# An SSM's tap matrix in eight transfers a layer instead of 32, and the rows of w_glu and p_ssm in two transfers a chunk, in another channel order

## The chip, the cores and the metric

The kernel runs on one core of one Trainium2 chip, in one launch. The metric is the device time of that launch in microseconds. All inputs lie in HBM at the start, in float32, and the output (1, 256, 1024) is written there.

## What is computed

Two post-norm decoder layers over 256 positions of width 1024. In each layer a hybrid mixer (an S5 state-space branch with a GLU, beside a sparse attention) and a SwiGLU feed-forward of width 2816, both modulated by a conditioning vector. The S5 branch has 32 groups of 16 channels and 64 complex states; w_glu is 512 x 512, p_ssm 512 x 1024. The change lies in this branch and in how these two weights are read for it. Cut to what matters:

```python
def s5_branch(u, lam_re, lam_im, log_dt, b_re, b_im, c_re, c_im, d_skip, w_glu, b_glu):
    uf = u.astype(f32).reshape(bsz, L, SSM_GROUPS, SSM_GROUP)
    ...
    _, _, hr, hi = lax.associative_scan(combine, (a_r, a_i, xr, xi), axis=1)
    y = (jnp.einsum('bsgp,gip->bsgi', hr, c_re.astype(f32))
         - jnp.einsum('bsgp,gip->bsgi', hi, c_im.astype(f32))
         + d_skip.astype(f32).reshape(SSM_GROUPS, SSM_GROUP) * uf)
    y = jax.nn.gelu(y.reshape(bsz, L, SSM_WIDTH))
    y = y * jax.nn.sigmoid(y @ w_glu.astype(f32) + b_glu.astype(f32))
    return y

def hybrid_mixer(u, ...):
    z = u @ w_in
    ...
    merged = jax.nn.sigmoid(g_ssm) * (y_ssm @ p_ssm) + jax.nn.sigmoid(g_attn) * (y_attn @ p_attn)
    return merged @ w_out
```

## The kernel before, in words

**Weights.** Nearly all of the time is matmuls with weights that are read once. SP issues the loads on one queue, in chunks of 512 KB: `w_in` as 128 partitions x 2 x 512, `w_cond` (for the modulation) as 128 x 1024. A class `Stream` holds the order of all chunks; `pump_dma` (L334) issues a chunk once one of six raw buffers is free, and `advance` (L354) has the chunks split, two ahead of the one in use. A chunk is split into a high part (ACT's cast, L388) and the rest (DVE's subtraction, L389), and PE multiplies three of the four products of parts: L1355 where the weights are the moving side, L1431 where they are stationary. `w_cond` goes to PE unsplit (L476). The order of PE's instructions is that of the program text; the order on ACT, DVE, POOL and SP is made by a scheduler from priorities and its own estimates, and is fixed in the program. Each engine takes its list strictly in order, and so does SP with its DMAs; a DMA waits on SP until the eighth one before it has landed.

**The S5 branch** (`ssm_run`, L762). Time is cut into 32 blocks of T = 8 positions. Groups are numbered by k (0 to 3, a block of 32 partitions) and m (0 to 7). Inside a block the output follows from the inputs of the block by a small Toeplitz matrix, the *taps*; between blocks a scan of states runs on DVE (L834 and L835 transpose for it on PE, L505 and L506 swap halves by DMA). `ssm_tables` leaves the kernel of the recurrence in an SBUF tile `KT`, 128 partitions x 1920, of which 16 rows of each 32 are channels. It is written to a DRAM copy `KT_d` in one transfer of 960 KB (L797), and read back into the tap matrix `MT` (128 rows: position s and channel j; then m, k and 128 columns) with an offset that shifts by 16 columns with s. That is `taps_in` (L799): for each k and each s one transfer of 16 partitions x 8 x 128, 64 KB in pieces of 512 bytes (L805), 32 a layer. PE uses `MT` at L865, after the scan (L861). Before it, `rope` (the input of the branch) is written to the tile `s` by 16x8x128 transfers from SBUF (L774) on SP's and ACT's queues.

Then GELU (L869 to L875), whose last product on DVE writes `yg` in the order t, m, i (i is the channel of a group), PE's transposes of it (L885), ACT's copy of them (L886, which writes with a stride of eight elements), the split into `yy` (L227 and L893), and the GLU on PE (`glu`, L896, matmuls L910 to L912).

**w_glu and p_ssm.** Their rows have to stand in the order of the transposes, so a chunk of theirs is read with `w_rows_perm` (L402) in eight transfers of 16 partitions x 2 x 512, 64 KB each (L349): 32 for w_glu and 64 for p_ssm in both layers. The columns of w_glu are permuted as well, by the split of such a chunk (ACT L384, DVE L385). The bias of the GLU is transposed from `bg4` (L530) into the same order.

**Beside it**, on PE: L821 (states into the blocks), L1011 (scores of the attention's indexer, from copies that ACT makes with L227), ACT's L1014 (their activation), L1044 and L1057 (further steps of the attention).

Of the kernel before, what the change touches and what calls it, by code (L numbers as in the profile page):

```python
# [8 lines left out]
F32 = mybir.dt.float32  # L9
# [14 lines left out]
T = 8  # L24
# [148 lines left out]
def kernel(  # L173
# [10 lines left out]
    dp = ctx.enter_context(tc.tile_pool(name="dp", bufs=1, space=DRAM))  # L184
    V, A, P, PE, SP = nc.vector, nc.scalar, nc.gpsimd, nc.tensor, nc.sync
# [21 lines left out]
    def nm(p):  # L207
        uid[0] += 1
        return f"{p}_{uid[0]}"

    def sbt(shape, tag, dt=F32, bufs=1):
        return sb.tile(shape, dt, tag=tag, bufs=bufs, name=nm(tag))
# [7 lines left out]
    def place(name, eng):  # L220

        n = placed[name] = placed.get(name, -1) + 1
        return {"V": V, "A": A}.get(PLACE.get((name, n)), eng)
# [8 lines left out]
    def tp_t():  # L232

        return ps.tile([128, 512], F32, tag="bk", bufs=3, name=nm("bk"))
# [9 lines left out]
    ident = K1[:, K_ID:K_ID + 128]  # L244
# [20 lines left out]
    class Task:  # L265
        def __init__(self, gen):
            self.gen, self.done, self.wait = gen, False, 0
            self.name = gen.__name__
            self.n = started[self.name] = started.get(self.name, -1) + 1
            self.i = 0  # L270
# [31 lines left out]
    class Chunk:  # L302


        def __init__(self, kind, src, shape, perm=False, by_part=False):
            self.kind, self.src, self.shape, self.perm, self.by_part = kind, src, shape, perm, by_part
            self.raw = self.hi = self.lo = None
            self.read = False
            self.ins = []
            self.lo_on = V  # L310
            self.place = None
# [11 lines left out]
    class Stream:  # L323
# [10 lines left out]
        def pump_dma(self, upto=10 ** 9):  # L334

            while self.nd < min(len(self.q), upto):
                ch = self.q[self.nd]
                whole = ch.kind == "raw" and len(ch.shape) == 2 and ch.shape[1] != 128
                ring, cap = (self.rings["whole"], 2 * NHL) if whole else (self.rings["raw"], NRAW)
                if len(ring) >= cap and not self.free(ring[-cap]):  # L340
                    break
                tag = ("hi", "lo")[len(ring) % 2] if whole else "raw"
                ch.raw = wp.tile([128, 1024], F32, tag=tag, bufs=NHL if whole else NRAW, name=nm(tag))
                ring.append(self.nd)
                v = ch.raw[:, 0:math.prod(ch.shape)]
                ch.rv = v if len(ch.shape) == 1 else v.rearrange("p (k n) -> p k n", k=ch.shape[0])
                if ch.by_part:
                    for m in range(8):
                        SP.dma_start(ch.rv[16 * m:16 * m + 16], ch.src[m])  # L349
                else:  # L350
                    SP.dma_start(ch.rv, ch.src)
                self.nd += 1
# [22 lines left out]
        def split(self, ch):  # L375
            nk, n = ch.shape
            hv = ch.hi[:, 0:nk * n].rearrange("p (k n) -> p k n", k=nk)
            lv = ch.lo[:, 0:nk * n].rearrange("p (k n) -> p k n", k=nk)
            if ch.perm:
                for k in range(nk):  # L380
                    src = ch.rv[:, k].rearrange("p (m k i) -> p k m i", m=8, k=4)
                    ho = hv[:, k].rearrange("p (k m i) -> p k m i", k=4, m=8)
                    lo = lv[:, k].rearrange("p (k m i) -> p k m i", k=4, m=8)
                    i = A.copy(ho, src)  # L384
                    j = place("lo", ch.lo_on).tensor_tensor(lo, src, ho.bitcast(F32), ALU.subtract)  # L385
                ch.ins = [i, j]
            else:
                i = A.copy(hv, ch.rv)  # L388
                j = place("lo", ch.lo_on).tensor_tensor(lv, ch.rv, hv.bitcast(F32), ALU.subtract)  # L389
                ch.ins = [i, j]  # L390
            ch.hv, ch.lv = hv, lv
# [4 lines left out]
    st = Stream()  # L396
# [4 lines left out]

    def w_rows_perm(w, k0, nk, c0, n):  # L402

        return w.rearrange("(m k i) n -> m i k n", k=4, i=16)[:, :, k0:k0 + nk, c0:c0 + n]

    class Block:

# [103 lines left out]
    def ssm_prep(l, w0, w, we):  # L511
        R = ssm[l]
        c0t = sbt([128, 1024], "c0")
# [15 lines left out]
        bg4 = c0t[0:4, 640:768]  # L529
        SP.dma_start(bg4.rearrange("k (m i) -> k m i", m=8), b_glu[l].rearrange("(m k i) -> k m i", m=8, k=4))  # L530
        yield w0
        V.tensor_copy(pr3[:, 2], ld.broadcast_to((32, 128)))
        t = tp_t()
        for i in range(3):
            PE.transpose(t[:, 32 * i:32 * i + 32], pr3[:, i], ident[0:32, 0:32])
        PE.transpose(t[:, 96:104], dt8.rearrange("m k i -> m (k i)"), ident[0:8, 0:8])
        PE.transpose(t[:, 104:108], bg4, ident[0:4, 0:4])
        prm = sbt([128, 108], "prm")
        A.copy(prm, t[:, 0:108])
        lr, li, ldt = prm[:, 0:32], prm[:, 32:64], prm[:, 64:96]  # L540
# [83 lines left out]
        c0t = sbt([128, 1024], "c0")  # L624
# [31 lines left out]
        for q in range(4):  # L656
# [25 lines left out]
            for h in range(2):  # L682
                t = tp_t()
# [78 lines left out]
    def ssm_run(l, acc, tab):  # L762
# [20 lines left out]
        uy = sbt([128, 2112], "p8")  # L783
        U = uy[:, 0:1024].rearrange("p (g c) -> p g c", g=G)
        R["y2"] = uy[:, 1024:2048].rearrange("p (k t) -> p k t", k=4)
        for h in range(2):
            t = tp_t()
# [3 lines left out]
        yield W_U  # L791
        while not tab.done:
            yield 0
        MT = sbt([128, 8, 4, 128], "MT")
        KT = R["KT"]
        KT_d = dp.tile([4, 32, 8, 240], F32, tag="KT_d", bufs=1, name=nm("KT_d"))
        SP.dma_start(KT_d.rearrange("k j m c -> (k j) m c"), KT)  # L797

        def taps_in():  # L799

            yield 4
            for k in range(4):

                for s in range(T):
                    SP.dma_start(MT[16 * s:16 * s + 16, :, k],  # L805
                                 bass.AP(tensor=KT_d.tensor, offset=KT_d.offset + k * 32 * 1920 + 16 * s,
                                         ap=[[1920, 16], [240, 8], [1, 128]]))
                yield 2

        t_taps = start(taps_in())  # L810
        yield
        E, BT, CT, ST, RH = R["E"], R["BT"], R["CT"], R["ST"], R["RH"]
        yg = uy[:, 1024:2048].rearrange("p (t m i) -> p t m i", t=T, m=8)
        w4s = [sbt([128, 4, 512], "s8"), sbt([128, 4, 512], "k8")]
        phase = [[a_[:, 16 * h:16 * h + 16].rearrange("p g c -> p (g c)") for a_ in (CT, ST, RH)] for h in range(2)]
        for h in range(2):
            p = tp_t()
# [10 lines left out]
        for h in range(2):  # L828
# [3 lines left out]
            p, q = tp_t(), tp_t()  # L832
# [22 lines left out]
        for h in range(2):  # L855
            S_, a_, r_, g_ = [w4s[h][:, i] for i in range(4)]
            py = tp_t()
            for m in range(4):
                for k in range(4):
                    gg = 4 * (4 * h + m) + k  # L860
                    PE.matmul(py[32 * k:32 * k + 32, 128 * m:128 * m + 128], g_[:, 32 * (4 * m + k):32 * (4 * m + k) + 32],  # L861
                              E[:, 128 * gg:128 * gg + 128], start=True, stop=False, tile_position=(0, 32 * k))
                for k in range(4):
                    gg = 4 * (4 * h + m) + k
                    PE.matmul(py[32 * k:32 * k + 32, 128 * m:128 * m + 128], U[:, gg], MT[:, 4 * h + m, k],  # L865
                              start=False, stop=True, tile_position=(0, 32 * k))

            q1, q2, ys = a_, r_, S_
            A.copy(ys, py)  # L869
            A.activation(q1, py, AF.Square)  # L870
            V.tensor_scalar(q1, q1, 0.044715, 1.0, ALU.mult, ALU.add)
            place("g1", V).tensor_tensor(q1, q1, ys, ALU.mult)
            A.activation(q2, q1, AF.Tanh, scale=GELU_C)
            V.tensor_scalar(q2, q2, 1.0, None, ALU.add)
            place("g2", V).tensor_tensor(yg[:, :, 4 * h:4 * h + 4].rearrange("p t m i -> p m t i"),  # L875
                            q2.rearrange("p (m t i) -> p m t i", m=4, t=T),
                            ys.rearrange("p (m t i) -> p m t i", m=4, t=T), ALU.mult)
            yield
# [3 lines left out]
        for h in range(2):  # L882
            t = tp_t()
            for i in range(4):
                PE.transpose(t[:, 128 * i:128 * i + 128], yg[:, 4 * h + i].rearrange("p m i -> p (m i)"), ident)  # L885
            A.activation(yTv[:, 4 * h:4 * h + 4], t.rearrange("p (t q) -> p t q", t=4), AF.Copy, scale=0.5)  # L886
        yield
        yy = sbt([128, 4, 4, 256], "MT", dt=F32R)
# [369 lines left out]
    def plan_chunk(blk, w, i, c0, perm_rows=False, perm_cols=False, k0=0, whole=False):  # L1258
        per = 4 if blk.n <= 256 else 2
        k = (per * i + k0) % blk.kts  # L1260
        nk = min(per, blk.kts - k)
        blk.first, blk.last = k0, (k0 - 1) % blk.kts
        src = w_rows_perm(w, k, nk, c0, blk.n) if perm_rows else w_rows(w, 128 * k, nk, c0, blk.n)
        blk.pos.append(len(st.q))
        blk.parts.append((k, nk))
        st.q.append(Chunk("raw" if whole else "mm", src, (nk, blk.n), perm_cols, perm_rows))

    def plan_block(w, kts, c0, n, conds=None, **kw):
        blk = Block(kts, n)
# [12 lines left out]
    for l in range(depth):  # L1282
# [30 lines left out]
        for j in range(6):  # L1313
            n = 512 if j < 5 else 256
# [11 lines left out]
        p = B[l, "wd", 1 if l + 1 < depth else 2].pos  # L1326
# [5 lines left out]
        if l:  # L1332
            p = B[l, "u"].pos
# [484 lines left out]
```

## Time and profile before

| | us |
|---|---|
| median of 3 runs | 964.92 (960.31 to 967.47) |
| the profiled execution | 964.36 |
| its span in the profile | 962.5 |
| around the span | 1.86 |
| PE busy | 886.3 (92%) |
| DVE busy | 671.3 (70%) |
| ACT busy | 403.6 (42%) |
| moved by DMA | 202.64 MB, 211 GB/s over the span |

The profile is of one execution. "Busy" counts instructions that compute; an engine that waits for a semaphore is idle. For an engine, a timeline gives each stretch of like instructions with the idle time before it and what ended that idle time. The granted clock is 1.00 at 2.4 GHz and 0.50 at 1.2 GHz. The DMA share is the mean busy share of the core's 16 DMA engines; beside the GB/s it tells whether they were full and slow or simply unused.

### The profile page before, as it was taken

To read this page: it belongs to the slowest core of one execution; us is meant where nothing else is said; L and a number is where in the kernel's file an instruction comes from. 1 tells how busy PE (TensorE), PEld (TensorE's weight loads), DVE (VectorE), ACT (ScalarE), POOL (GpSimd) and SP (SyncE) were. 2 spreads that over 40 slices of the span, in tenths; PEclk is the share of its full clock that TensorE was granted. 3 is DMA by queue.
4 is the path that set the end of the run, shared out by engine and by line. 5 is a ranking of instruction groups with operands and counts; after the bars stand their busy time and mean duration, and the time that the engine had idled before them with its cause. 6 is when DMAs were issued, how large, how long until landed. Compare 5 with 4: busy or idle time off the path is not lost.

```text
span 962.5 us, 16427 instructions
## 1 busy us (share of the span) xinstructions
PE 886.3 (92%) x6419; PEld 749.6 (78%) x6419; DVE 671.3 (70%) x1187; ACT 403.6 (42%) x600; POOL 16.2 (2%) x42
## 2 busy tenths in 40 slices
PE   5849988999978999999999889999999999999996
PEld 4437756897767688889887676689888789999896
DVE  4468969865487557678867886995669776555564
ACT  2114324563353353335443542456536154444340
POOL 1000000000000000000000000000000000000002
PEclk9969998999988999999999989999999999999999
DMA  9946777677695388888566297757468265565641
GB/s 260 303 126 209 227 226 266 197 257 220 235 304 156 121 264 288 293 300 288 190 204 224 69 258 222 250 184 247 147 208 265 99 208 184 179 192 181 197 132 44
DMA packets 123989, 202.64 MB, mean 211 GB/s; under 512 B 11960, under 2 KB 52864, under 8 KB 123912
## 3 DMA queue, kind: packets, MB, share of 16 engines
q1 hardware_dynamic: 122328, 200.11, 65.3%
q10 hardware_dynamic: 1584, 1.48, 0.5%
q8 instruction: 50, 0.82, 0.3%
q14 instruction: 27, 0.22, 0.1%
HBM read 195.38 MB, written 3.03 MB: 206 GB/s over the span
## 4 chain that ended last, share of the span: by engine, by line
PE 48%; DMA 9%; DVE 5%; issue 3%; ACT 2%; POOL 1%; SPq 0%; POOLq 0%; ACTq 0%; DVEq 0%
PE acc L1431 25%; PE acc L1355 17%; DMA raw<-in_w_gate_up_dram 5%; DMA raw<-in_w_in_dram 2%; DVE lo L389 2%; PE cnd L476 1%; ACT hi L388 1%; DMA raw<-in_w_down_dram 1%; DMA KT_d<-k 1%; PE bk L1153 1%; PE bk L1080 1%; PE bk L1113 1%; POOL mv L1224 0%; DVE BT L389 0%; DVE rope L1161 0%
## 5 line engine op out<-in xcount | busy, mean ns | idle before, releaser
L389 DVE TENSOR_TENSOR lo<-raw,hi 128x1024 fp32r<-128x1024 f32 (+2 forms) x217 | 262.3, 1213 | 176.3 <-ACT hi L388 168.0
L388 ACT CAST hi<-raw 128x1024 fp32r<-128x1024 f32 (+2 forms) x217 | 225.0, 1042 | 335.6 <-PE acc L1431 81.7
L1431 PE MATMUL acc<-aTh,hi 128*128 128x256 f32 x832 | 138.0, 288 | 1.2 <-ACT hi L388 1.2
L1431 PE MATMUL acc<-aTh,lo 128*128 128x256 f32 x832 | 133.0, 282 | 1.0 <-DVE lo L389 1.0
L1431 PE MATMUL acc<-aTl,hi 128*128 128x256 f32 x832 | 132.6, 281 | 0.0
L1431 PEld LDWEIGHTS acc<-aTh,hi 128*128 128x128 f32 x832 | 113.6, 189 | 21.5 <-issue 14.7
L1431 PEld LDWEIGHTS acc<-aTh,lo 128*128 128x128 f32 x832 | 113.4, 189 | 1.5 <-DVE lo L389 1.5
L1431 PEld LDWEIGHTS acc<-aTl,hi 128*128 128x128 f32 x832 | 113.5, 189 | 0.0
L1355 PE MATMUL acc<-hi,aTh 128*128 128x512 f32 (+2 forms) x200 | 64.6, 408 | 9.6 <-ACT aTh L1664 5.5
L1355 PE MATMUL acc<-hi,aTl 128*128 128x512 f32 (+2 forms) x200 | 60.9, 389 | 4.8 <-DVE aTl L1665 3.7
L1355 PE MATMUL acc<-lo,aTh 128*128 128x512 f32 (+2 forms) x200 | 60.4, 387 | 0.2 <-DVE lo L389 0.2
L1355 PEld LDWEIGHTS acc<-hi,aTh 128*128 128x128 f32 x200 | 34.9, 195 | 24.5 <-issue 9.0
L1355 PEld LDWEIGHTS acc<-hi,aTl 128*128 128x128 f32 x200 | 36.9, 191 | 14.3 <-DVE aTl L1665 4.8
L1355 PEld LDWEIGHTS acc<-lo,aTh 128*128 128x128 f32 x200 | 37.3, 193 | 8.2 <-DVE lo L389 0.4
L476 PE MATMUL cnd<-raw,csil 128*32 128x512 f32 x320 | 43.3, 616 | 0.0
L1355 PE MATMUL acc<-lo,MT 128*128 128x512 f32 (+1 forms) x144 | 36.4, 350 | 0.6 <-DVE lo L389 0.6
L1355 PE MATMUL acc<-hi,MT 128*128 128x512 f32 (+1 forms) x144 | 36.8, 352 | 0.0
L1355 PE MATMUL acc<-hi,q 128*128 128x512 f32 (+1 forms) x144 | 36.3, 349 | 0.0
L1355 PEld LDWEIGHTS acc<-lo,MT 128*128 128x128 f32 x144 | 24.0, 188 | 4.9 <-DVE lo L389 1.0
L1355 PEld LDWEIGHTS acc<-hi,q 128*128 128x128 f32 x144 | 24.1, 188 | 3.9
L1355 PEld LDWEIGHTS acc<-hi,MT 128*128 128x128 f32 x144 | 23.8, 188 | 3.4
L685 PE MATMUL bk<-K,c 128*128 128x128 f32 x64 | 10.2, 288 | 16.0 <-DVE c L680 16.0
(374 smaller groups left out, 1391.3 us busy)
## 6 DMA issues: line engine op xcount, KB each, us to landing
raw<-in_w_cond_dram SPq DMA_DIRECT2D x96, 512.0 KB, 6.1
raw<-in_w_gate_up_dram SPq DMA_DIRECT2D x88, 512.0 KB, 4.9
raw<-in_w_in_dram SPq DMA_DIRECT2D x62, 512.0 KB, 4.6
raw<-in_w_down_dram SPq DMA_DIRECT2D x43, 512.0 KB, 3.8
raw<-in_p_attn_dram SPq DMA_DIRECT2D x16, 512.0 KB, 4.9
raw<-in_w_out_dram SPq DMA_DIRECT2D x16, 512.0 KB, 4.7
MT<-KT_d SPq DMA_DIRECT2D x64, 64.0 KB, 3.1
raw<-in_p_ssm_dram SPq DMA_DIRECT2D x64, 64.0 KB, 2.3
```

What stands on the lines that cost most here:

```text
L388: i = A.copy(hv, ch.rv)
L389: j = place("lo", ch.lo_on).tensor_tensor(lv, ch.rv, hv.bitcast(F32), ALU.subtract)
L476: PE.matmul(acc[32 * g:32 * g + 32], csil[:, kt], rv[:, 512 * (g % 2):512 * (g % 2) + 512], start=kt == 0, stop=kt == KD - 1, tile_positio ...
L685: PE.transpose(t[:, 128 * i:128 * i + 128], c0q[:, 512 * h + 128 * i:512 * h + 128 * i + 128], ident)
L1080: PE.matmul(p[:, nk * (h - h0):nk * (h - h0) + nk], X["qT"][:, 4 * kv + h, 128 * t:128 * t + 128], X["kT"][:, kv, 0:nk], start=True, stop= ...
L1113: PE.matmul(p, X["V"][:, s, 128 * kv:128 * kv + 128], PT[:, s].rearrange("p h q -> p (h q)"), start=s == 0, stop=s == t)
L1153: PE.transpose(p[:, 128 * k:128 * k + 128], X[:, t, 128 * kt:128 * kt + 128], ident)
L1355: PE.matmul(o, st_of(kt, t)[part == 2], (ch.lv if part == 1 else ch.hv)[:, k, :], start=kt == blk.first and part == 0, stop=kt == blk.last ...
L1431: PE.matmul(acc[:, 256 * i:256 * i + 256], w[:, k, n:n + 128], mov(kt)[part == 2], start=kt == blk.first and part == 0 and i == 0, stop=kt ...
```

## The change

Three things are done.

1. `KT_d` is laid out channel by channel (16, 4, 1920) and written by four transfers of 16 x 1920 (120 KB each), the 16 rows of each block of 32 that are channels. The taps come back in eight transfers a layer, one for each s: 16 partitions x 32 x 128, 256 KB, in pieces of 512 bytes as before. `MT` has k ahead of m.
2. The rows of w_glu and p_ssm stand in the order i, m instead of m, i. A chunk is read in two transfers of 128 partitions x 1 x 512 (256 KB).
3. So the channels of the GLU have that order too: the split of w_glu (L384, L385) and the GELU's last product (L875) write with a stride of eight elements, the transposes (L885) read without one, and the bias is put in order by one more DVE copy of 4x128 a layer, ahead of its transpose.

```diff
-                if ch.by_part:
-                    for m in range(8):
-                        SP.dma_start(ch.rv[16 * m:16 * m + 16], ch.src[m])
+                if len(ch.src.shape) == 4:
+                    for k in range(ch.shape[0]):
+                        SP.dma_start(ch.rv[:, k], ch.src[:, :, k])
...
-                    ho = hv[:, k].rearrange("p (k m i) -> p k m i", k=4, m=8)
-                    lo = lv[:, k].rearrange("p (k m i) -> p k m i", k=4, m=8)
+                    ho = hv[:, k].rearrange("p (k i m) -> p k m i", k=4, m=8)
+                    lo = lv[:, k].rearrange("p (k i m) -> p k m i", k=4, m=8)
...
-        return w.rearrange("(m k i) n -> m i k n", k=4, i=16)[:, :, k0:k0 + nk, c0:c0 + n]
+        return w.rearrange("(m k i) n -> i m k n", k=4, i=16)[:, :, k0:k0 + nk, c0:c0 + n]
...
+        bgi = c0t[0:4, 768:896]
+        V.tensor_copy(bgi.rearrange("k (i m) -> k i m", m=8), bg4.rearrange("k (m i) -> k i m", m=8))
...
-        MT = sbt([128, 8, 4, 128], "MT")
+        MT = sbt([128, 4, 8, 128], "MT")
         KT = R["KT"]
-        KT_d = dp.tile([4, 32, 8, 240], F32, tag="KT_d", bufs=1, name=nm("KT_d"))
-        SP.dma_start(KT_d.rearrange("k j m c -> (k j) m c"), KT)
+        KT_d = dp.tile([16, 4, 1920], F32, tag="KT_d", bufs=1, name=nm("KT_d"))
+        for k in range(4):
+            SP.dma_start(KT_d[:, k], KT[32 * k:32 * k + 16].rearrange("j m c -> j (m c)"))
...
-            for k in range(4):
-                for s in range(T):
-                    SP.dma_start(MT[16 * s:16 * s + 16, :, k],
-                                 bass.AP(tensor=KT_d.tensor, offset=KT_d.offset + k * 32 * 1920 + 16 * s,
-                                         ap=[[1920, 16], [240, 8], [1, 128]]))
-                yield 2
+            for s in range(T):
+                SP.dma_start(MT[16 * s:16 * s + 16].rearrange("p k m c -> p (k m) c"),
+                             bass.AP(tensor=KT_d.tensor, offset=KT_d.offset + 16 * s,
+                                     ap=[[7680, 16], [240, 32], [1, 128]]))
+                if s % 2:
+                    yield 2
...
-            place("g2", V).tensor_tensor(yg[:, :, 4 * h:4 * h + 4].rearrange("p t m i -> p m t i"),
+            place("g2", V).tensor_tensor(yg[:, :, :, 4 * h:4 * h + 4].rearrange("p t i m -> p m t i"),
...
-                PE.transpose(t[:, 128 * i:128 * i + 128], yg[:, 4 * h + i].rearrange("p m i -> p (m i)"), ident)
+                PE.transpose(t[:, 128 * i:128 * i + 128], yg[:, 4 * h + i].rearrange("p i m -> p (i m)"), ident)
```

The order of PE and of POOL stays as it was. On SP, in the first layer, from the write of `KT_d` on (`raw<-in_w_in_dram` and `raw<-in_w_cond_dram` are chunks of weights), before:

```order
L797 DMA KT_d_1019<-k_156_752 128x1920
L351 DMA raw_1004<-in_w_in_dram 128x2x512
L805 DMA MT_1018<-KT_d_1019 16x8x128 x4
L351 DMA raw_1006<-in_w_in_dram 128x2x512
L805 DMA MT_1018<-KT_d_1019 16x8x128 x9
L351 DMA raw_1008<-in_w_cond_dram 128x1024
L351 DMA raw_1010<-in_w_cond_dram 128x1024
L351 DMA raw_1138<-in_w_in_dram 128x2x512
L805 DMA MT_1018<-KT_d_1019 16x8x128 x2
L351 DMA raw_1140<-in_w_in_dram 128x2x512
L805 DMA MT_1018<-KT_d_1019 16x8x128 x14
L351 DMA raw_1142<-in_w_cond_dram 128x1024
```

and after:

```order
L801 DMA KT_d_1020<-k_156_753 16x1920 x4
L808 DMA MT_1019<-KT_d_1020 16x32x128 x2
L351 DMA raw_1005<-in_w_in_dram 128x2x512
L808 DMA MT_1019<-KT_d_1020 16x32x128 x3
L351 DMA raw_1007<-in_w_in_dram 128x2x512
L808 DMA MT_1019<-KT_d_1020 16x32x128 x3
L351 DMA raw_1009<-in_w_cond_dram 128x1024
L351 DMA raw_1011<-in_w_cond_dram 128x1024
L351 DMA raw_1142<-in_w_in_dram 128x2x512
L351 DMA raw_1144<-in_w_in_dram 128x2x512
L351 DMA raw_1146<-in_w_cond_dram 128x1024
L351 DMA raw_1148<-in_w_cond_dram 128x1024
```

The eight taps now stand in three groups ahead of the two chunks of w_cond, where 13 of the 32 stood before; none is left behind the third chunk of w_in.

The same place of SP's list in the second layer, before:

```order
L351 DMA raw_5426<-in_w_in_dram 128x2x512
L805 DMA MT_5571<-KT_d_5572 16x8x128
L351 DMA raw_5466<-in_w_in_dram 128x2x512
L805 DMA MT_5571<-KT_d_5572 16x8x128 x3
L351 DMA raw_5487<-in_w_cond_dram 128x1024
L805 DMA MT_5571<-KT_d_5572 16x8x128
L351 DMA raw_5557<-in_w_cond_dram 128x1024
L805 DMA MT_5571<-KT_d_5572 16x8x128 x6
L351 DMA raw_5727<-in_w_in_dram 128x2x512
L805 DMA MT_5571<-KT_d_5572 16x8x128 x4
L351 DMA raw_5729<-in_w_in_dram 128x2x512
L805 DMA MT_5571<-KT_d_5572 16x8x128 x17
```

and after:

```order
L801 DMA KT_d_5517<-k_817_5193 16x1920 x3
L351 DMA raw_5371<-in_w_in_dram 128x2x512
L351 DMA raw_5411<-in_w_in_dram 128x2x512
L808 DMA MT_5516<-KT_d_5517 16x32x128 x3
L351 DMA raw_5432<-in_w_cond_dram 128x1024
L808 DMA MT_5516<-KT_d_5517 16x32x128 x2
L351 DMA raw_5502<-in_w_cond_dram 128x1024
L808 DMA MT_5516<-KT_d_5517 16x32x128 x3
L351 DMA raw_5669<-in_w_in_dram 128x2x512
L351 DMA raw_5671<-in_w_in_dram 128x2x512
L505 DMA s_874_5534<-s_874_5534 64x512
```

Two chunks of w_in now go ahead of all taps, and the third and fourth come behind the last tap, where 11 and 15 taps of 32 stood ahead of them. The swaps of halves (L505, L506) follow them directly.

On ACT, at the GLU of the first layer (`L384` splits w_glu, `L886` copies the transposes, `L227 CAST MT` begins the split of `yy`), before:

```order
L384 CAST hi_1787<-raw_1693 128x512 x2
L886 ACTIVATE p_180_919<-bk_1669 128x4x128
L886 ACTIVATE p_180_919<-bk_1675 128x4x128
L227 CAST MT_1743<-p_180_919 128x1024
L384 CAST hi_1793<-raw_1702 128x512 x2
```

and after (L886 is L890 there):

```order
L384 CAST hi_1755<-raw_1673 128x4x8x16 x2
L384 CAST hi_1761<-raw_1676 128x4x8x16 x2
L890 ACTIVATE p_180_920<-bk_1649 128x4x128
L890 ACTIVATE p_180_920<-bk_1655 128x4x128
L227 CAST MT_1711<-p_180_920 128x1024
```

The second pair of casts now stands ahead of the copies of the transposes.

## Rows read from the trace of the kernel before

**Rows 1.** The page: busy us, share of the span and instructions of each engine.

```profile
PE 886.3 (92%) x6419; PEld 749.6 (78%) x6419; DVE 671.3 (70%) x1187; ACT 403.6 (42%) x600; POOL 16.2 (2%) x42
```

**Rows 2.** Timeline of PE: start us, us, engine, line, op, tiles, count [idle before <-releaser].

```profile
117.40 1.16 PE L1011 MATMUL bk<-kiT,q 64*128 64x128 f32 x14 [1.12 <-ACT s L227]
...
125.88 0.33 PE L834 MATMUL bk<-K,s 128*128 128x128 f32 x1 [4.33 <-ACT sp L1014]
...
161.96 1.12 PE L1057 MATMUL bk<-K,rope 128*128 128x128 f32 x4 [3.97 <-ACT sp L1014]
...
596.06 1.16 PE L1011 MATMUL bk<-kiT,q 64*128 64x128 f32 x16 [0.90 <-ACT q L227]
...
603.34 0.42 PE L861 MATMUL bk<-E,s 128*32 128x128 f32 x8 [3.12 <-DVE q L227]
```

**Rows 3.** Windows: us, then busy (x count) PE, PEld, DVE, ACT, POOL; clock, DMA share, GB/s.

```profile
160.70:167.50 6.80, 5.54 (x55) 5.17 (x58) 6.17 (x20) 4.95 (x8) 0.00 (x0) 0.50 0.63 215
...
170.00:265.00 95.00, 94.44 (x733) 79.31 (x732) 58.31 (x108) 44.87 (x84) 0.73 (x3) 1.00 0.71 229
...
612.00:740.00 128.00, 128.00 (x958) 113.44 (x958) 97.62 (x176) 70.52 (x116) 0.00 (x0) 1.00 0.61 201
```

**Rows 4.** Timeline of ACT, first layer, around the first two PE waits.

```profile
112.14 1.05 ACT L388 CAST hi<-raw 128x1024 fp32r<-128x1024 f32 x1 [3.18 <-DMA raw<-in_w_in_dram]
...
116.76 0.59 ACT L227 COPY s<-bk 128x512 f32<-128x512 f32 x1 [3.30 <-DVE s L227]
...
124.29 1.04 ACT L388 CAST hi<-raw 128x1024 fp32r<-128x1024 f32 x1 [6.45 <-DMA raw<-in_w_in_dram]
...
139.04 1.05 ACT L388 CAST hi<-raw 128x1024 fp32r<-128x1024 f32 x1 [10.27 <-DMA raw<-in_w_in_dram]
```

**Rows 5.** Timeline of SP, first layer: issues of taps and of w_in.

```profile
105.51 2.50 SPq L805 DMA_DIRECT2D MT<-KT_d  x4
...
118.24 12.44 SPq L805 DMA_DIRECT2D MT<-KT_d  x14
...
133.91 0.90 SPq L351 DMA_DIRECT2D raw<-in_w_in_dram  x2
```

**Rows 6.** The line that issues the taps: duration ns min/median/max; last row from issue to landing.

```profile
L805 SPq DMA_DIRECT2D MT<-KT_d x64: 538/597/1498, 105.5 to 587.4; - x64
...
DMA to landing us min/median/max: 2.6/3.1/8.8
```

**Rows 7.** Windows, the same columns: two with transfers into 16 partitions, one with 128.

```profile
89.00:90.00 1.00, 1.00 (x8) 0.86 (x7) 1.00 (x10) 0.67 (x2) 0.00 (x0) 1.00 1.03 130
...
584.00:588.00 4.00, 4.00 (x19) 3.19 (x18) 2.26 (x4) 0.00 (x0) 0.00 (x0) 1.00 0.42 100
...
600.00:605.00 5.00, 1.81 (x19) 0.75 (x22) 3.88 (x8) 2.02 (x3) 0.00 (x0) 0.94 1.04 392
```

**Rows 8.** Timelines of the second layer: SP's issues, PE and ACT.

```profile
562.27 0.58 SPq L805 DMA_DIRECT2D MT<-KT_d  x1
...
589.41 1.09 SPq L351 DMA_DIRECT2D raw<-in_w_in_dram  x2
...
583.45 0.74 PE L1355 MATMUL acc<-hi,aTh 128*128 128x512 f32 x2
...
593.38 1.05 ACT L388 CAST hi<-raw 128x1024 fp32r<-128x1024 f32 x1 [9.77 <-DMA raw<-in_w_in_dram]
```

**Rows 9.** Around the GLU: ACT and PE in the first layer, then lines L384, L385, L886.

```profile
179.90 1.14 ACT L384 CAST hi<-raw 128x512 fp32r<-128x512 f32 x2 [6.44 <-DMA raw<-in_ssm_w_glu_dram]
...
188.29 0.39 PE L910 MATMUL acc<-MT,hi 128*128 128x256 f32 x1
...
L384 ACT CAST hi<-raw x8: 614/617/622, 179.9 to 656.0; 128x512 fp32r<-128x512 f32 x8
...
L385 DVE TENSOR_TENSOR lo<-raw,hi x8: 674/683/693, 180.6 to 657.3; 128x512 fp32r<-128x512 f32 x8
...
L886 ACT ACTIVATE p<-bk x4: 1196/1236/1313, 180.9 to 628.9; 128x512 f32<-128x512 f32 x4
```

More of the change, by code (lines that the diff above doesn't have):

```diff
@@ L302, with __init__ @@
     class Chunk:
-        def __init__(self, kind, src, shape, perm=False, by_part=False):
-            self.kind, self.src, self.shape, self.perm, self.by_part = kind, src, shape, perm, by_part
+        def __init__(self, kind, src, shape, perm=False):
+            self.kind, self.src, self.shape, self.perm = kind, src, shape, perm
             self.raw = self.hi = self.lo = None
@@ L536, in ssm_prep @@
         PE.transpose(t[:, 96:104], dt8.rearrange("m k i -> m (k i)"), ident[0:8, 0:8])
-        PE.transpose(t[:, 104:108], bg4, ident[0:4, 0:4])
+        PE.transpose(t[:, 104:108], bgi, ident[0:4, 0:4])
         prm = sbt([128, 108], "prm")
@@ L812, in ssm_run @@
         E, BT, CT, ST, RH = R["E"], R["BT"], R["CT"], R["ST"], R["RH"]
-        yg = uy[:, 1024:2048].rearrange("p (t m i) -> p t m i", t=T, m=8)
+        yg = uy[:, 1024:2048].rearrange("p (t i m) -> p t i m", t=T, m=8)
         w4s = [sbt([128, 4, 512], "s8"), sbt([128, 4, 512], "k8")]
@@ L864, in ssm_run @@
                     gg = 4 * (4 * h + m) + k
-                    PE.matmul(py[32 * k:32 * k + 32, 128 * m:128 * m + 128], U[:, gg], MT[:, 4 * h + m, k],
+                    PE.matmul(py[32 * k:32 * k + 32, 128 * m:128 * m + 128], U[:, gg], MT[:, k, 4 * h + m],
                               start=False, stop=True, tile_position=(0, 32 * k))
@@ L1265, in plan_chunk @@
         blk.parts.append((k, nk))
-        st.q.append(Chunk("raw" if whole else "mm", src, (nk, blk.n), perm_cols, perm_rows))
+        st.q.append(Chunk("raw" if whole else "mm", src, (nk, blk.n), perm_cols))
     def plan_block(w, kts, c0, n, conds=None, **kw):
```

## The prediction

> **What bounds the kernel now.** I read the busy times first: PE works for 886.3 of 962.5 us [rows 1]. The reader is to see there that only some 76 us are left for PE to wait in, and that an edit gains only if it shortens one of those waits, or the half clock that follows a wait. Then PE's own order of time, for the waits in the stretches that the change touches [rows 2]: before the matmuls of L1011 at 117.40 (1.12 us), L834 at 125.88 (4.33), L1057 at 161.96 (3.97) in the first layer, and L1011 at 596.06 (0.90) and L861 at 603.34 (3.12) in the second. That is 13.4 us. Behind three of them the granted clock is 0.50, that is 1.2 GHz and not 2.4: for 6.8 us from 160.70 [rows 3], and for 3.4 us each from 126.5 and from 604.4. Half of these 13.6 us, 6.8, is lost. Elsewhere PE has no hole that this change could fill: it is busy for 94.44 of the 95 us from 170 and for all of the 128 us from 612 [rows 3], where w_glu and p_ssm are read.
>
> Next, why PE waits. The releasers named for L1011 and L834 are ACT copies, but ACT itself stood still: at 124.29 it waited 6.45 us for a chunk of w_in, and the activation that L834 needs came right behind that cast [rows 4]. ACT takes its list in order, so a late chunk holds back what has nothing to do with it. Why the chunk is late is on SP [rows 5]: one queue issues w_in, w_cond and the taps, a tap transfer takes 0.60 us of it [rows 6], and 14 of them in a row (118.24, 12.44 us) stand ahead of two further chunks of w_in at 133.91, whose cast had ACT wait 10.27 us [rows 4]. The second layer is the same: 17 taps in a row, two chunks behind them at 589.41, an ACT wait of 9.77 us [rows 8].
>
> **The taps, the part that decides.** Removed: 32 transfers of 64 KB a layer, 32 x 0.597 = 19.1 us of SP. Added: 8 of 256 KB, at the same or somewhat longer issue about 5 us. So SP stops being the limit, and the question is how long one 256 KB transfer holds the 16 DMA engines that all loads share. It lands in only 16 partitions, in 512 B pieces like before. The trace has no such transfer, so I bound it by two rows [rows 7]:
> - From 584 to 588 only 64 KB taps are under way: 100 GB/s at a DMA share of 0.42, that is 238 GB/s while an engine carries. 262,144 B then take 1.1 us.
> - From 89 to 90 transfers of the shape 16x8x128 from rope to s (the line L774; 16 partitions, the same pieces) follow closely: the engines are full (1.03) and move 130 GB/s, where 128-partition loads move 392 at the same share. Then one tap takes 2.0 us.
>
> I take 2.0. The 64 KB taps come 0.6 us apart and the engines rest in between, so they show a short burst; four times as many bytes in one piece are nearer to the crowded row. Against it: that row holds a second stream.
>
> The Trainium skill (SBUF — State Buffer, "Door 1: The DMA port swizzle (why [64,N] ≈ [32,N])") says that the rate of a transfer goes by how many of 16 ports its partitions reach; 16 neighbouring ones reach 4. Of the 435 GB/s that it gives for all, that is an estimate of 109 GB/s and 2.4 us a tap, and by it the sum below would be 971. The crowded row agrees in kind, the spaced one (238 GB/s) does not.
>
> *First layer.* Now the order is two taps, chunk a, three taps, chunk b, three taps, two of w_cond, c, d, two of w_cond, e. The write of KT_d has half the bytes (16 rows of each 32) but four issues, also of 16 partitions; I leave its end at 105.51, when the first tap issued before [rows 5] (983,040 B took 2.5 us at 392 GB/s; 491,520 B take 1.3 at that rate and 3.8 at 130). From an issue to the landing of a single tap it takes 2.6 us at least [rows 6], 2.3 of it not data. A 512 KB chunk takes 1.34 us at 392 GB/s. Landings, in order through the queue: a 105.5 + 2.3 + 4.0 + 1.3 = 113.1; b, three taps on, 120.5; c, after three taps and two of w_cond, 130.5; e 135.9. What follows:
> - ACT's cast of b (1.05) ends at 121.6 instead of 113.2 [rows 4], and the copy for L1011, at 116.76 before, comes behind it: PE resumes at 122.2 for 117.40, 4.8 later.
> - The cast of c starts at 130.5 for 124.29; L834 followed 1.59 after it, so 132.1 for 125.88, 6.2 later. Two waits stay, and longer.
> - But e is there 3.1 us before 139.04. The wait before L1057 ended at 161.96 with ACT behind a chunk of the same queue, so what came then comes at 158.9. PE arrives at 157.99 + 6.2 = 164.2 and finds it: that wait is gone. Net 164.2 - 161.96 = +2.2. The clock I leave (two waits before, two after).
>
> *Second layer.* Two chunks of w_in now go ahead of all taps, which costs nothing. The third waits behind eight taps and two of w_cond: with KT_d landed at 562.27 [rows 8], 562.3 + 2.3 + 16.0 + 2.7 + 1.3 = 584.6. Its cast ends at 585.7; PE used it at 583.45 without waiting, so +2.2 is a new wait. The swaps and the next two chunks follow at once, the first of them near 588.7 (swaps 1.4, chunks 1.3 each) instead of 593.38: 4.7 earlier, and the waits of 0.90 and 3.12 go. Net -1.8; the clock again as it was.
>
> **w_glu and p_ssm.** 72 issues of SP go, of 96. No PE wait lies there (94.44 of 95 us, 128 of 128), so nothing is gained; without that cover it would be the 6.44 us that ACT waits for w_glu at 179.90 [rows 9].
>
> **The new order of channels.** The cast of L384 now writes with a stride of eight elements. A row for that is L886, which writes so already: 1236 ns, against 617 for L384 [rows 9]. So 4 x 0.62 = 2.5 us more of ACT a layer. In the first layer it stands where it can hurt: the second pair of w_glu casts now goes ahead of L886, so the chain 4 x 1.24 + 2 x 1.24 + 1.05 (a cast of 128x1024) leads to PE's L910 at 188.29. From 179.90 that ends at 188.4, and a DVE step follows; w_glu lands earlier, since 4 issues take the place of 16. I put 0.5, between 0 and 1.7. On DVE eight products of L385 and four of L875 write with that stride, with no row for it: between nothing (683 ns now) and double as on ACT, 0.7 us more each; PE's full stretches cover either. The added copy of 4x128 stands at the start among loads; nothing.
>
> **Sum.** +2.2 - 1.8 + 0.5 = +0.9 on the profiled run's 964.36, which stands 0.06% under the median: 965.3 us.
>
> **Rivals.**
> - *Taps run freely* (1.1 us each). For: the spaced row. Against: the crowded one. Then b lands at 116.0 and c at 123.3, L834 starts 1.0 us sooner, e lands at 128.7, ten before it did, and the wait of 3.97 and its half clock (3.4) go: first layer -8.4. The third chunk of the second layer lands at 577.4, in time: -4.0 and half of 3.4, -5.7. With +0.5: -13.6, 951 us. The Trainium skill speaks for this side too (DMA: Bandwidth & Descriptors, "Rules for kernel authors"): merge small transfers; no row here prices that.
> - *Taps clog the queue, slower than before.* One mechanism: a tap needs 2.6 us (262,144 B at the 100 GB/s that the spaced stream has as its mean), and ACT, in order, waits on b, then c, in the first layer, and the third chunk of the second comes late. By the same steps: L834 at 136.9 (+11.0), e at 140.7, so nothing is given back but the wait of 3.97: +7.0; second layer 590.5 for 583.45, +7.0 - 4.0 = +3.0; 1.7 more at half clock, 0.5 for glu: +12.2, 977 us. It adds 16 us for each us a tap takes longer, so it passes 1% from about 2.5 us.
> - *SP was not what held the chunks*: then neither the issue times nor the new order matter, and the time stays. For: a tap needs 2.6 us at least to land, but up to 8.8 [rows 6], so it came into a crowded queue. It ends where the forecast does.
>
> **How the numbers follow.** A measurement here tells about 1%, 9.6 us, from no change. Forecast (taps at 1.5 to 2.5 us) 0.50 and the third rival 0.07, all within 1%: 0.57. Free taps: 0.25, faster. Clogged: 0.18, slower. The range takes in both ends, 950 to 977; the likeliest case alone spans 957 to 973.
>
> **What would show it.** In the changed trace: a tap's landing (2.0 us of data gives 3 to 5 us alone and more in the queue); DMA share near 1 at 130 to 200 GB/s while only taps fly, against 240 and more if they run freely; ACT's casts of b and c near 120 and 130; PE waits before L1011 and L834 longer, the one before L1057 gone; in the second layer a new wait near 583 and none at 595 to 603; L384 near 1.24 us. If L834 starts before 125, the rate is wrong and the second figure falls to 951; if L1057 still waits, the giving back is wrong, and it is slower.

## The result, and the profile after

The changed kernel takes 977.1 us (median of four runs, 968.01 to 982.36) against 966.19 for the kernel before on the same chips (960.31 to 967.62). The ratio is 1.0113 with a 95% interval of 1.0064 to 1.0162: slower, by about 1%; the interval does not reach 1. The profiled execution took 974.27 us, its span is 972.5, 10.0 more than before. The forecast was 965.3, and the range ended at 977.0: the median lies just outside it, the profiled execution inside. One run of e8 below (1105.93 us) went at a lower clock than all the others and is left out of e8's figures.

From the page after, PE's busy time, the queue that carries nearly all loads, and the issues of the taps (KB each, us to landing):

```profile
PE 885.3 (91%) x6419; PEld 749.9 (77%) x6419; DVE 677.8 (70%) x1189; ACT 406.9 (42%) x600; POOL 16.6 (2%) x42
...
q1 hardware_dynamic: 120376, 199.12, 67.6%
...
MT<-KT_d SPq DMA_DIRECT2D x16, 256.0 KB, 15.2
```

PE works as long as in [rows 1]; what was added is waiting. The queue holds the engines for 67.6% of the span, with 1 MB less to move. A tap lands 15.2 us after its issue (the median).

PE's own order, the matmuls that answer to [rows 2] (L1011 is L1015 here, L834 and the L835 that follows it are L838 and L839, L1057 is L1061, L861 is L865; L989, the one that waits at 598.27 as L993, had no wait before):

```profile
119.10 0.46 PE L1015 MATMUL bk<-kiT,q 64*128 64x128 f32 x2 [3.10 <-DVE q L227]
...
130.64 2.07 PE L1015 MATMUL bk<-kiT,q 64*128 64x128 f32 x14 [11.08 <-ACT s L227]
...
137.54 0.27 PE L838 MATMUL bk<-K,s 128*128 128x128 f32 x1
...
138.88 0.33 PE L839 MATMUL bk<-K,s 128*128 128x128 f32 x1 [1.06 <-ACT sp L1018]
...
170.45 0.66 PE L1061 MATMUL bk<-K,rope 128*128 128x128 f32 x4 [1.19 <-ACT sp L1018]
...
598.27 0.44 PE L993 MATMUL bk<-K,rope 128*128 128x128 f32 x2 [2.15 <-ACT kiT L227]
...
610.87 0.43 PE L865 MATMUL bk<-E,s 128*32 128x128 f32 x8 [2.48 <-DVE q L227]
```

The indexer's scores, which had waited 1.12 us, wait 3.10 and then 11.08. L838 comes 11.7 us later than L834 did (125.88) and no longer waits; a wait of 1.06 stands before the next one, L839. L1061 comes 8.5 us later than L1057: part is given back, as the wait there shrinks from 3.97 to 1.19. In the second layer the last of these matmuls comes at 610.87 for 603.34, with a wait of 2.48 that had been 3.12.

What ACT waited for, in the lines that answer to [rows 4] and to the last of [rows 8]:

```profile
115.66 1.04 ACT L388 CAST hi<-raw 128x1024 fp32r<-128x1024 f32 x1 [9.43 <-DMA raw<-in_w_in_dram]
...
125.72 1.04 ACT L388 CAST hi<-raw 128x1024 fp32r<-128x1024 f32 x1 [9.02 <-DMA raw<-in_w_in_dram]
...
137.28 1.05 ACT L388 CAST hi<-raw 128x1024 fp32r<-128x1024 f32 x1 [6.21 <-DMA raw<-in_w_in_dram]
...
596.73 1.04 ACT L388 CAST hi<-raw 128x1024 fp32r<-128x1024 f32 x1 [12.55 <-DMA raw<-in_w_in_dram]
```

The casts of a, b and c start at 115.66, 125.72 and 137.28, where b and c had started at 112.14 and 124.29. ACT stands in order behind each, as before, only longer. SP, which issued 32 taps at 0.6 us, now issues three in 7.71 us, because each of its transfers waits for an earlier one to land; the two chunks of w_cond behind them take 3.90. The chunk e of the forecast is issued only at 141.75:

```profile
111.44 7.71 SPq L808 DMA_DIRECT2D MT<-KT_d  x3
...
119.25 3.90 SPq L351 DMA_DIRECT2D raw<-in_w_cond_dram  x2
...
141.75 2.35 SPq L351 DMA_DIRECT2D raw<-in_w_in_dram  x2
```

```profile
L808 SPq DMA_DIRECT2D MT<-KT_d x16: 538/624/4269, 105.6 to 579.5; - x16
...
DMA to landing us min/median/max: 13.5/15.2/16.8
```

And the windows (us, busy of PE, PEld, DVE, ACT, POOL, then clock, DMA share, GB/s), in the columns of [rows 7]:

```profile
107.00:108.00 1.00, 1.00 (x7) 0.83 (x6) 1.00 (x5) 0.00 (x0) 0.00 (x0) 1.00 0.83 188
...
108.00:111.00 3.00, 3.00 (x19) 1.52 (x17) 1.57 (x6) 0.00 (x0) 0.00 (x0) 1.00 1.28 104
...
112.00:113.20 1.20, 1.20 (x7) 0.97 (x6) 0.00 (x0) 0.00 (x0) 0.00 (x0) 1.00 0.97 106
...
113.20:114.50 1.30, 1.30 (x20) 0.85 (x23) 0.00 (x0) 0.00 (x0) 0.00 (x0) 1.00 1.04 349
...
116.00:120.00 4.00, 0.46 (x3) 0.29 (x2) 2.89 (x6) 0.70 (x1) 0.00 (x0) 1.00 1.25 97
...
120.00:137.10 17.10, 6.46 (x25) 5.28 (x26) 7.37 (x13) 2.39 (x4) 0.00 (x0) 0.50 1.15 199
...
168.00:180.00 12.00, 10.81 (x174) 9.23 (x164) 11.44 (x34) 8.40 (x13) 0.00 (x0) 1.00 0.64 214
...
175.00:273.00 98.00, 97.32 (x758) 82.39 (x758) 66.97 (x121) 51.50 (x91) 0.73 (x3) 1.00 0.73 237
...
620.00:748.00 128.00, 126.75 (x952) 112.27 (x951) 100.52 (x176) 71.51 (x115) 0.00 (x0) 1.00 0.63 200
```

While only taps fly (108 to 111, 116 to 120), the engines are shown as more than full at 104 and 97 GB/s. So 262,144 B take 2.5 to 2.7 us, not the 2.0 that the forecast took. Only the first microsecond of them is quick: 188 GB/s at a share of 0.83 from 107 to 108, that is 227 while an engine carries. The chunk of w_in behind the taps starts as slowly as they run (106 until 113.2) and goes on at 349. The granted clock is 0.50, 1.2 GHz, for the whole 17.1 us from 120, after PE had waited 3.10 us and begun to wait 11.08 more. The last two windows cover the reading of w_glu and p_ssm: PE is busy for 97.32 of 98 and for 126.75 of 128 us, nearly as in [rows 3]; the 1.25 that are missing in the second are one wait, at 635.22.

### The profile page after: what moved, and what is told of

It reads as the page before. It is cut to its first block, busy times and chain, and to the rows that moved or that the text cites. A ratio compares the mean times of both kernels' runs of the same rounds, so it can differ in the third digit from the quotient of the medians.

```text
span 972.5 us, 16226 instructions
## 1 busy us (share of the span) xinstructions
PE 885.3 (91%) x6419; PEld 749.9 (77%) x6419; DVE 677.8 (70%) x1189; ACT 406.9 (42%) x600; POOL 16.6 (2%) x42
## 3 DMA queue, kind: packets, MB, share of 16 engines
q1 hardware_dynamic: 120376, 199.12, 67.6%
## 4 chain that ended last, share of the span: by engine, by line
PE 42%; DMA 10%; DVE 9%; issue 3%; ACT 2%; POOL 1%; SPq 0%; POOLq 0%; ACTq 0%; DVEq 0%
PE acc L1435 24%; PE acc L1359 13%; DMA raw<-in_w_gate_up_dram 5%; DMA raw<-in_w_in_dram 3%; DVE lo L389 3%; ACT hi L388 2%; DMA raw<-in_w_down_dram 1%; PE cnd L476 1%; DVE rope L1165 1%; PE bk L1084 1%; PE bk L1157 1%; DMA raw<-in_w_out_dram 1%; PE bk L1117 1%; DMA s<-rope 0%; POOL mv L1228 0%
## 5 line engine op out<-in xcount | busy, mean ns | idle before, releaser
L1216 DVE SCALAR_TENSOR_TENSOR tmp<-c,acc 128x512 f32<-128x512 f32 (+1 forms) x18 | 11.1, 625 | 20.1 <-PE acc L1359 16.7
## 6 DMA issues: line engine op xcount, KB each, us to landing
MT<-KT_d SPq DMA_DIRECT2D x16, 256.0 KB, 15.2
```

The source lines that it names most:

```text
L1216: V.scalar_tensor_tensor(q, gtb[:, s], 1.0, acc[:, 0:n], ALU.add, ALU.mult)
```

## The experiments

Two theories and a third were put against each other. A: a transfer into 16 partitions runs at a quarter of the rate that 128 partitions get, and fills the queue while it does. B: the strided casts and the later copies of the transposes cost the time. C: the order (taps ahead of w_in), the narrow writes of the copy, or the re-reading of a small copy costs it, whatever the target.

**e1, e2: the change in two halves.** e1 is the changed kernel with the taps as before; e2 the kernel before with the new taps alone.

```diff
-            SP.dma_start(KT_d[:, k], KT[32 * k:32 * k + 16].rearrange("j m c -> j (m c)"))
+        SP.dma_start(KT_d.rearrange("k j m c -> (k j) m c"), KT)
...
-            for s in range(T):
+            for k in range(4):
+                for s in range(T):
```

> The changed kernel with the taps as before (32 transfers of 64 KB a layer, one write of the copy); the new reading of w_glu and p_ssm and the new channel order stay. Theory A (a transfer into 16 partitions runs at about 105 GB/s and fills the queue: the taps alone cost the time): within 4 us of the kernel before, 962 to 970 us, and the wait before L1011 again about 1 us. Theory B (the strided casts and the later copies of the transposes cost it): 972 to 980 us.

> The kernel before with the new taps alone. Theory A: as slow as the changed kernel, 972 to 982 us, taps landing 13 to 17 us after their issue. Theory B: 962 to 970 us.

e1: 962.24 us against 963.82, ratio 0.9985 (0.9963 to 1.0006). e2: 975.34, ratio 1.0122 (1.0082 to 1.0163). In e1 PE waits 0.38 us before the scores. PE's waits in e2 (L1013 is the indexer's scores, L837 a transpose for the scan) are those of the changed kernel:

```profile
118.33 0.46 PE L1013 MATMUL bk<-kiT,q 64*128 64x128 f32 x2 [2.94 <-DVE q L227]
...
129.77 2.07 PE L1013 MATMUL bk<-kiT,q 64*128 64x128 f32 x14 [10.99 <-ACT s L227]
...
138.70 0.33 PE L837 MATMUL bk<-K,s 128*128 128x128 f32 x1 [1.74 <-ACT sp L1016]
```

So the taps alone cost the time, and B falls. e2's taps landed 11 us after issue, less than I expected; the time came out as expected.

**e3: the same taps into all partitions.** The copy is laid out by blocks of 16 columns, then channel, so that row 16 s + j of `MT` begins 512 elements after the one before it, and a transfer can take all 128 rows at once. Eight transfers of 256 KB stay; the pieces are 512 bytes in the first layer and 2 KB in the second.

```diff
-        KT = sbt([128, 8, 240], "k8")
+        KT = sbt([128, 15, 8, 16], "k8")
...
-        MT = sbt([128, 4, 8, 128], "MT")
+        MT = sbt([128, 8, 4, 8, 16], "MT")
...
-        KT_d = dp.tile([16, 4, 1920], F32, tag="KT_d", bufs=1, name=nm("KT_d"))
+        KT_d = dp.tile([15, 16, 4, 128], F32, tag="KT_d", bufs=1, name=nm("KT_d"))
...
+                    SP.dma_start(MT[:, u:u + 4, k].rearrange("p u m i -> p u (m i)"),
+                                 bass.AP(tensor=KT_d.tensor, offset=KT_d.offset + 8192 * u + 128 * k,
+                                         ap=[[512, 128], [8192, 4], [1, 128]]))
```

> The changed kernel with the copy of the kernel of the recurrence laid out block by block (15 blocks of 16 columns, then channel), so that each of the eight tap transfers of 256 KB goes to all 128 partitions: in pieces of 512 bytes in the first layer, 2 KB in the second. SP's list is nearly that of the changed kernel. Theory A (the partitions of the target set the rate): 240 to 390 GB/s while taps fly, landing 3 to 8 us, no long wait before the indexer's scores, and 950 to 958 us, faster than before. Theory C (the order, taps ahead of w_in, or the narrow writes of the copy, or re-reading a small copy, is what costs): 970 to 980 us and landing over 10 us.

953.36 us, ratio 0.9897 (0.9871 to 0.9923): faster than both kernels, with the taps in nearly the same places of SP's list. Windows with taps alone (first layer; second layer, once the two chunks of w_in ahead of the taps are through), and the wait that is left:

```profile
106.00:110.00 4.00, 4.00 (x20) 3.19 (x20) 4.00 (x19) 0.49 (x2) 0.00 (x0) 1.00 0.70 197
...
559.50:561.50 2.00, 0.37 (x13) 0.28 (x16) 1.77 (x3) 1.87 (x3) 0.00 (x0) 1.00 1.03 353
```

```profile
123.33 2.07 PE L1022 MATMUL bk<-kiT,q 64*128 64x128 f32 x14 [6.64 <-ACT s L227]
```

In the second layer the taps run at 353 GB/s. In the first they leave the engines idle for a third of the time (0.70) and move 197, so 281 GB/s while they carry. The waits of 14 us are one of 6.64, which theory A had not expected. C falls as far as order, re-reading and the narrow writes go (e3 too writes its copy in four transfers from 16 partitions); that e3 also lays the copy out differently is what e6 is for.

**e4, e5: 32 and 64 partitions.** e4 takes the changed kernel's copy, where the source then has the pair or the four of s as its outermost dimension; e5 takes e3's copy, where the partitions are outermost.

```diff
-                             bass.AP(tensor=KT_d.tensor, offset=KT_d.offset + 16 * s,
-                                     ap=[[7680, 16], [240, 32], [1, 128]]))
+                             bass.AP(tensor=KT_d.tensor, offset=KT_d.offset + 16 * s,
+                                     ap=[[16, n], [7680, 16], [240, 32], [1, 128]]))
```

and e5, against e3:

```diff
+            n = 32 if l == 0 else 64
+            for r in range(0, 128, n):
+                SP.dma_start(MT[r:r + n].rearrange("p u k m i -> p u (k m i)"),
+                             bass.AP(tensor=KT_d.tensor, offset=KT_d.offset + 512 * r,
+                                     ap=[[512, n], [8192, 8], [1, 512]]))
```

> The changed kernel with four transfers of 32 partitions (512 KB) in the first layer and two of 64 partitions (1 MB) in the second. Theory A with the port rule (64 neighbouring partitions reach no more ports than 32): 200 to 220 GB/s in both layers while only taps fly. A rate in proportion to the partitions instead: about 210 in the first, about 390 in the second. Theory C (the source sets the rate): about 105 in both. The time by theory A 955 to 967 us, by theory C 970 to 980 us.

> The block-wise copy of e3 again (pieces of 2 KB, the transfer's outermost dimension is the partitions, so all 16 engines can share it), read in four transfers of 32 partitions (512 KB) in the first layer and two of 64 partitions (1 MB) in the second. Theory A with the port rule: 200 to 220 GB/s in both layers while only taps fly. A rate in proportion to the partitions: about 210 in the first, 390 in the second. Theory C (the source sets the rate): the same rate as e3 showed for 2 KB pieces, 340 to 390 GB/s, in both. Time 955 to 970 us by theory A.

e4 came out as no theory expected: 1032.76 us, ratio 1.0716. Its windows (first layer, n = 2; second layer, n = 4):

```profile
116.00:128.00 12.00, 0.00 (x0) 0.00 (x0) 0.00 (x0) 0.00 (x0) 0.00 (x0) 0.58 0.14 41
...
606.00:638.00 32.00, 6.55 (x92) 5.33 (x90) 3.64 (x10) 2.05 (x4) 0.13 (x1) 0.66 0.30 54
```

The DMA share is 0.14 and 0.30, at 41 and 54 GB/s: as if about two, and four or five, of the 16 engines worked. It tells nothing on ports. e5, one run, took 960.98 us; its windows with taps only (32 partitions, then 64):

```profile
110.00:112.00 2.00, 2.00 (x13) 0.95 (x13) 0.92 (x3) 0.00 (x0) 0.00 (x0) 1.00 1.05 197
...
565.00:572.00 7.00, 1.50 (x33) 1.23 (x34) 6.00 (x12) 4.25 (x7) 0.00 (x0) 0.68 1.05 208
```

197 and 208 GB/s with full engines: 64 neighbouring partitions get hardly more than 32, and both about twice what 16 get. That is what the port rule forecast; a rate in proportion to the partitions and one set by the source did not.

**e6: 16 and 128 partitions with the same copy and pieces.** e5 with n = 16 in the first layer and 128, a single transfer of 2 MB, in the second.

```diff
-            n = 32 if l == 0 else 64
+            n = 16 if l == 0 else 128
```

> The same copy and the same pieces of 2 KB, in eight transfers of 16 partitions (256 KB) in the first layer and a single one of 128 partitions (2 MB) in the second. Theory A: about 105 GB/s in the first layer (long waits before the indexer's scores, as in the changed kernel) and 340 to 400 in the second. If the 512-byte pieces had been the cause, the first layer runs at 300 or more. Time by theory A 960 to 972 us.

One run, 964.21 us; in the first layer PE again waits 2.00 and 9.09 us before the scores. The windows (16, then 128):

```profile
116.00:120.00 4.00, 2.16 (x66) 1.69 (x64) 2.20 (x5) 1.04 (x1) 0.00 (x0) 1.00 1.06 118
...
574.00:577.00 3.00, 1.89 (x64) 1.62 (x64) 3.00 (x5) 3.00 (x6) 0.00 (x0) 1.00 1.00 353
```

118 GB/s at a share of 1.06 in the first, 353 in the second, with the same copy, bytes and pieces of 2 KB. So the number of partitions that one transfer reaches makes the difference, and neither the piece nor the copy. The order holds within a layer, too: 118, 197 and 281 (while they carry) for 16, 32 and 128 partitions in the first layer (e6, e5, e3), 208 and 353 for 64 and 128 in the second (e5, e6).

**e7, e8: another queue.** e7 is e3's layout with pieces of 2 KB and the taps issued by POOL; e8 is the changed kernel with its narrow taps issued by POOL.

```diff
-                SP.dma_start(MT[16 * s:16 * s + 16].rearrange("p k m c -> p (k m) c"),
+                P.dma_start(MT[16 * s:16 * s + 16].rearrange("p k m c -> p (k m) c"),
```

> e3 with 2 KB pieces in both layers and the tap transfers issued by POOL on its own queue, so that none stands ahead of w_in on SP's. If what is left in e3 (6.64 us before the indexer's scores) is w_in waiting in line behind the taps: 943 to 951 us, that wait under 3 us. If it is the amount of bytes or the later casts: 951 to 956 us.

> The changed kernel, 16 partitions a transfer, with the taps on POOL's queue. If a slow write into few ports holds the DMA engines themselves, the chunks of w_in on the other queue are slow too: 968 to 980 us, DMA share near 1 at 150 to 250 GB/s between 105 and 125. If it holds only the queue behind it: 945 to 958 us, no long wait before the indexer's scores.

e7: 950.82 us, ratio 0.9852 (0.9813 to 0.9891), the fastest median here, though its interval and e3's overlap. The wait before the scores, 6.64 in e3, is gone (0.16). That was w_in standing in line behind the taps: the two chunks that e3 issues at 107.15 and 112.41, behind four and seven taps, e7 issues together at 103.69. The first layer's pieces went from 512 B to 2 KB as well, so how much of the time each of the two gave is not told apart:

```profile
116.72 1.16 PE L1016 MATMUL bk<-kiT,q 64*128 64x128 f32 x14 [0.16 <-ACT s L227]
```

```profile
103.69 2.56 SPq L351 DMA_DIRECT2D raw<-in_w_in_dram  x2
```

e8: 972.71 us (median of nine runs), ratio 1.0077 (1.0045 to 1.0108), still slower than before. Two windows of the first layer; the queues in the first of them (packets, MB, share of the 16 engines; q0 is POOL's); SP's issue of c; the casts of b and c; and PE's wait:

```profile
111.00:121.00 10.00, 9.42 (x110) 7.05 (x103) 9.20 (x19) 2.39 (x4) 0.92 (x2) 1.00 1.03 104
...
122.00:132.00 10.00, 0.00 (x0) 0.00 (x0) 0.00 (x0) 0.00 (x0) 0.00 (x0) 0.60 1.01 159
```

```profile
q0 software_dynamic: 316, 1.04, 103.3%
```

```profile
112.76 2.28 SPq L351 DMA_DIRECT2D raw<-in_w_in_dram  x2
```

```profile
112.33 1.05 ACT L388 CAST hi<-raw 128x1024 fp32r<-128x1024 f32 x1 [3.36 <-DVE q L227]
...
135.68 1.04 ACT L388 CAST hi<-raw 128x1024 fp32r<-128x1024 f32 x1 [17.66 <-DMA raw<-in_w_in_dram]
```

```profile
137.27 0.48 PE L839 MATMUL bk<-K,s 128*128 128x128 f32 x1 [15.43 <-ACT sp L1018]
```

b is early now (112.33), but c, issued at 112.76, was cast only at 135.68, after a wait of 17.66 us, although only two chunks of w_cond, and no tap, stand right ahead of it on its queue. From 111 to 121 POOL's queue is the only one that moves anything. The engines are full at 104 and 159 GB/s: the narrow write holds the engines, whichever queue it is on. The wait of PE only moved, from the scores to L839 (15.43 us).

## Why the prediction was wrong

The step that failed is the price of a tap, "I take 2.0". It was read from one window of 1 us at 130 GB/s in which a second stream was moving too, and the prediction said so. The two windows with taps alone show 104 and 97 GB/s, 2.5 to 2.7 us. The Trainium skill's figure (SBUF — State Buffer, "Door 1: The DMA port swizzle (why [64,N] ≈ [32,N])"), from which 2.4 us was an estimate, was nearer than my row. The other bound, 1.1 us, came from transfers of 64 KB with pauses between them. The changed kernel runs at that rate too, but for one microsecond (227 GB/s while an engine carries, against 238); the mean of the spaced row, 100 GB/s, is what packed taps get.

The mechanism of the first layer was right: chunks of w_in come late behind the taps, and ACT and then PE wait for them. The sum is sensitive to this one term: the prediction gave 16 us for each us of a tap, so 2.6 instead of 2.0 turns +0.9 into +10.5, 975 us. The profiled run took 974.27. The rival "taps clog the queue" (2.6 us, 977) is what happened; it had 0.18. That both totals come so close is luck in part, as the terms do not agree: the rival had +7.0 and +3.0 for the two layers and 2.2 for clock and GLU, and the trace shows +6.0 up to the first GLU, +1.4 from 547.70 to 610.87, and 2.5 behind.

Point by point:
- *First layer.* b and c were forecast to be cast near 120 and 130 and came at 125.72 and 137.28; L1061 came 8.5 us late, for +2.2. The prediction's steps with 2.6 us give 114.3, 123.5 and 135.3 for a, b and c, still 2 us early; 1.4 of these are there at a already (115.66), and what they are no run shows. Two steps failed beside the price. PE did not resume right behind the cast of b: the copy for the scores waits for a DVE copy ([rows 4] show it) and came 4.3 us after that cast, 4.6 before. So the long wait came ahead of the scores, and the one ahead of L834, which was to grow, went. And e, which was to come 3.1 us early and take away the wait before L1057, was issued at 141.75 and cast at 148.06, 9 us late. That wait shrank (3.97 to 1.19) because PE itself came later.
- *The clock.* The forecast left it as it was. It was at 0.50 before, ahead of the row in [rows 3]:

```profile
126.50:129.90 3.40, 3.40 (x17) 1.44 (x15) 3.40 (x8) 1.50 (x2) 0.13 (x1) 0.50 0.41 101
```

The new stretch at 0.50 is long, 17.1 us, but PE was busy for 6.46 of it, so 3.2 us at most are lost, where before 3.40 busy us from 126.5 and 5.54 from 160.70 [rows 3] lost 4.5 by the same reckoning. Behind L1061 the clock is now 1.00 (168 to 180), and so the 8.5 us have become 6.0 at the GLU, which began at 188.29 [rows 9] and now begins at 194.28:

```profile
194.28 0.39 PE L914 MATMUL acc<-MT,hi 128*128 128x256 f32 x1
```

- *Second layer.* The new wait was forecast near 583 with 2.2 us and came at 598.27 with 2.15, behind the third chunk, which ACT waited 12.55 us for. That the sizes meet is luck: the taps took longer, and the forecast had PE use that chunk too early. What answers to its 583.45 runs at 590.26 without a wait, 6.5 us before the chunk is cast (596.73):

```profile
590.26 0.73 PE L1359 MATMUL acc<-hi,aTh 128*128 128x512 f32 x2
```

- The wait at 610.87 did not go (2.48 of 3.12). So the -1.8 was wrong: a group of PE's transposes ahead of this stretch (L1153, now L1157) and the matmuls of the recurrence behind it (603.34, now 610.87) are 1.4 us farther apart than before. The first of them, in the chains of waits of the kernel before and of the changed one:

```profile
541.59 1.06 PE bk L1153 x8
```

```profile
547.70 1.08 PE bk L1157 x8
```

- *w_glu, p_ssm and the channel order.* Nothing gained, nothing lost: right, by e1. The lines that answer to [rows 9]:

```profile
L384 ACT CAST hi<-raw x8: 1156/1247/1304, 184.8 to 661.8; 128x512 fp32r<-128x512 f32 x8
...
L385 DVE TENSOR_TENSOR lo<-raw,hi x8: 1120/1200/1259, 186.0 to 663.2; 128x512 fp32r<-128x512 f32 x8
...
L879 DVE TENSOR_TENSOR p<-s x2: 1111/1152/1194, 177.6 to 622.7; 128x512 f32<-128x512 f32 x2
```

L384 takes 1247 ns, as forecast from L886 (1236). On DVE the strided write costs 1200 and 1152 ns where the contiguous one took 683, inside the bounds of nothing and double; PE's full stretches cover it. The one wait there, 1.25 us at 635.22, is not theirs: e2, which writes without a stride, has 1.02 us at that place, and e1, which writes with it, has none:

```profile
635.22 0.33 PE L889 MATMUL bk<-K,p 128*128 128x128 f32 x1 [1.25 <-ACT sp L1018]
```

What stays open: about 2.5 us of the 10 lie behind the matmuls at 610.87 (7.5 have come about by then). The trace shows them in the main as this wait and as a clock of 0.55 from 754.5 to 758.2, where the same stretch of the kernel before (745 to 749) had 1.00. e2 has both and e1 neither, so they come with the taps, as far as one profile of each tells; by what way no run shows.

```profile
754.50:758.20 3.70, 3.70 (x10) 2.94 (x11) 1.58 (x3) 0.00 (x0) 0.00 (x0) 0.55 0.88 288
```

## What to carry to other kernels

Count the partitions that a transfer reaches before merging transfers: eight large ones into 16 partitions each were worse than 32 small ones, although both moved about 100 GB/s while only taps flew: the small ones left the engines free in between (a DMA share of 0.42 against 1.25), and a slow transfer holds the engines for every queue. When a merge is wanted, lay the DRAM copy out so that one transfer reaches all 128 partitions, and keep the partitions as the outermost dimension. And a rate read from a burst or from a mixed window of 1 us is no rate to put a sum on; if the sum changes by 16 us for each us of it, the range has to carry the whole distance.

## What the hardware showed that was not expected

- 32 and 64 neighbouring partitions get nearly one rate, 197 and 208 GB/s (e5), 16 get 97 to 118 (after, e6), 128 get 353 (e6, e3). The Trainium skill's port rule, named above, says so, and these runs agree with it.
- An outermost dimension of 2 or 4 leaves most DMA engines unused: shares of 0.14 and 0.30 at 41 and 54 GB/s (e4), 69 us more than before in all. The Trainium skill (DMA: Bandwidth & Descriptors, "Rules for kernel authors") tells authors to keep a multiple of 16 outermost, as the slowest dimension limits the engines; e4 agrees.
- The profile's DMA share goes to 1.28 while narrow taps hold the engines, at 104 GB/s. A share at or over 1 at a low rate is the sign to look for.
